# Last down projection of a two-layer encoder trunk: 8 of 22 pairs of k-tiles by Strassen's algorithm

## The chip, the cores and the metric

The kernel runs on one core of a Trainium2 chip. The core has a matrix engine (TensorE, "PE" in the profile, its weight loads "PEld"), a vector engine (VectorE, "DVE"), a scalar engine (ScalarE, "ACT"), GpSimd ("POOL"), a queue processor for DMAs (SyncE, "SP") and 16 DMA engines. Data lie in an on-chip memory of 128 partitions; TensorE writes into eight accumulator banks (PSUM) of 128 partitions by 512 float32 numbers each. The metric is the device time of one execution in microseconds (us); lower is better.

## The reference, cut to what matters

Two layers, 256 tokens, 2048 features, all in float32. Each layer ends in a gated feed-forward block; after the second layer the result is normalised. The last product and what follows it:

```python
D_MODEL, SEQ, D_FF = 2048, 256, 5632
def conv_ffn(h, w_up, conv_w, conv_b, w_down):
    ...
    return (jax.nn.gelu(acc) * b) @ w_down          # [256, 5632] @ [5632, 2048]
...
        x = x + conv_ffn(rmsnorm(x, g_ffn[l]), w_up[l], conv_w[l], conv_b[l], w_down[l])
    return rmsnorm(x, g_final)
```

## The kernel before

**Three passes for one product.** Each float32 operand is held as the exact sum of two parts of 12 significant bits, hi and lo, in a type that TensorE multiplies at full rate, and hi·hi + hi·lo + lo·hi is accumulated in PSUM. Weights come from memory as float32 and are split on the chip: `fetch` (line 98) issues one DMA of 512 KB on SP's queue, which brings a tile `raw` of two k-tiles (2 x 128 rows) by 512 columns; `split_w` rounds it on ACT into `hi` (line 108) and subtracts on DVE to get `lo` (line 109). There are five buffers for `raw`, three for `hi` and three for `lo` (`wraw`, `wspl`), seven of 128x512 for passing results (`tmp`), and an arena of 30 units of 4 KB per partition for everything that lives longer.

**The stage around the change** is the down projection of the second layer. Its left operand, `gT`, is 22 units; each holds two k-tiles of 128 features by 256 tokens, hi and lo. Tokens go on the partitions of the result: two token tiles (`t`) of 128. The 2048 output columns are taken in four blocks of 512 (`for n in range(NB)`, line 601). For each block `rows` (line 122) goes through the 22 pairs of k-tiles: one fetch, one split, then for each k-tile `j` and token tile `t` three matmuls of 128x128 by 128x512 (`rows_mms`, lines 117 to 119), 12 matmuls to a fetched tile, 1056 in the stage. A block takes two banks of the six that `acc_banks` gives out in pairs; the last block takes the two banks of `tp_bank`, and in its last four pairs the first token tile goes ahead of the second (`late=4`), so that the first one's ending lies beside the second one's products.

**Before the stage** the residual `xT`, which has features on partitions, is transposed by TensorE through the two `tp` banks (line 597), and DVE copies it to `xb` (line 598), which needs units of the arena. **After each block** DVE adds the bank to the residual (line 607), ACT sums the squares (line 609), and GpSimd multiplies with the gain of the final norm (line 611; the gain is fetched by a DMA that GpSimd issues, line 603). At the end, for each token tile, DVE finishes the mean (618), GpSimd raises it to the power -1/2 (619), DVE multiplies the last block with its gain (620), and DVE and ACT scale the four blocks and have them stored (624 to 628).

**What sets the order.** The framework puts the instructions of each engine into one list, in which they run in order; it goes by the order of the program text and by when buffers and inputs come free. An instruction waits for its inputs, and for a buffer that another one still reads.

Of the kernel before, what the change touches and what calls it, by code (L numbers as in the profile page):

```python
# [17 lines left out]
P = 128  # L18
# [23 lines left out]
def trunk_kernel(ctx, tc, x, g_mix, w_in, b_forget, g_sgu, w_spatial, b_spatial,  # L42
                 w_branch_a, w_branch_b, w_out, g_ffn, w_up, conv_w, conv_b,
                 w_down, g_final, out):
    """Every float32 product with a weight matrix runs as three float32r passes: each operand is
    the exact sum of two parts of 12 significant bits, hi and lo, and hi*hi + hi*lo + lo*hi
    is accumulated in PSUM. The RMS factor of a token is applied to the products, since it is
    one number per token; the gain goes into the transposed operand."""
# [73 lines left out]
    def rows(w2d, c0, cols, ops, late=0):  # L122
        """Products with tokens on the partitions: per token tile [token, cols]. In the last `late`
        chunks the first token tile goes ahead of the second."""
        n = len(ops)
        if late:
            acc = [tp_bank()[:, :cols] for _ in range(NT)]
        else:
            acc = acc_banks()
            acc = [acc[:, t, :cols] for t in range(NT)]  # L130
        held = []
        for m in range(n):
            hi, lo = split_w(fetch(w2d, 2 * m, 2, c0, cols), more=2 < n - m <= late)
# [38 lines left out]
    def gained(src, gains):  # L172
        """[feature, 2, token] times a gain per feature, as an operand."""
# [20 lines left out]
    def inv_rms(sq):  # L194
        """Sums of squares by feature -> [P, NT] by token, 1/sqrt(mean + eps)."""
# [9 lines left out]
    def spread(inv):  # L205
        """[P, NT] by token -> [P, 2, T], the same on every partition and twice."""
# [8 lines left out]
    def params(l):  # L215
        """Gains, conv weights and forget bias; gain() and rest() lay them out with channels on partitions."""
# [40 lines left out]
    def sgu_weights(raw):  # L257
        """The lower triangles of the spatial weights, transposed."""
# [31 lines left out]
    # ---- the first loads and products: x is transposed ahead of the chunk that needs it; until it  # L290
    # is there, products of ones keep the tensor engine's clock up ----
# [49 lines left out]
    for l in range(DEPTH):  # L341
# [191 lines left out]
        def residual(w2d, ops, sq, gains):  # L533
            """xT += w2d^T ops; its squares; its product with the gains as operands."""
# [57 lines left out]
    xb = [unit([NT, 512]) for _ in range(NB)]  # L592
    for m in range(KT // 2):
        tp = tp_bank()
        for k in range(2):
            for t in range(NT):
                nc.tensor.transpose(tp[:, (2 * t + k) * P:(2 * t + k + 1) * P], xT[m][:, k, t * P:(t + 1) * P], ident)
        nc.vector.tensor_copy(xb[m // 2][:, :, m % 2 * T:m % 2 * T + T], tp.rearrange("p (t c) -> p t c", t=NT))
    ss = small.tile([P, NT, NB], F32, tag="ss", name=nm("ss"))
    fin = small.tile([P, NT], F32, tag="fin", name=nm("fin"))  # L600
    for n in range(NB):
        gf = scratch([P, 512])
        nc.gpsimd.dma_start(gf, g_final[None, n * 512:(n + 1) * 512].broadcast_to([P, 512]))
        acc = rows(w_down[DEPTH - 1], n * 512, 512, gT, late=4 if n == NB - 1 else 0)
        for t in range(NT):
            z = xb[n][:, t, :]
            nc.vector.tensor_tensor(z, acc[t], z, op=ALU.add)
            junk = scratch([P, 512])
            nc.scalar.activation(junk, z, AF.Square, accum_out=ss[:, t, n:n + 1])
            if n < NB - 1:  # L610
                nc.gpsimd.tensor_tensor(z, z, gf, op=ALU.mult)
        if n == NB - 2:
            nc.vector.tensor_reduce(fin, ss[:, :, 0:NB - 1], axis=AX.X, op=ALU.add)
            nc.vector.tensor_scalar(fin, fin, 1.0 / D, EPS, op0=ALU.mult, op1=ALU.add)
    for t in range(NT):
        f_ = fin[:, t:t + 1]
        z = xb[NB - 1][:, t, :]
        nc.vector.scalar_tensor_tensor(f_, ss[:, t, NB - 1:NB], 1.0 / D, f_, op0=ALU.mult, op1=ALU.add)
        nc.gpsimd.tensor_tensor(f_, f_, mhalf[:, 0:1], op=ALU.pow)
        nc.vector.tensor_tensor(z, z, gf, op=ALU.mult)  # L620
# [37 lines left out]
```

## Time and profile before

| | |
|---|---|
| median of 3 runs | 2717.66 us (2717.29 to 2719.5) |
| the profiled execution, first to last instruction | 2717.0 us |
| of it, the last down projection, first to last matmul | 2465.63 to 2707.51 us |
| TensorE, DVE, ACT, GpSimd busy over the span | 99%, 60%, 48%, 19% |
| weight tiles fetched for the two down projections | 176, 512 KB each |

The profile is that of one execution. Its page gives each engine's busy time, the chain of work that ended last, and the costliest groups of instructions by line of the kernel. Answers from the trace give single instructions: start and duration in us, engine, line, operation, what it writes and reads, the shape, and in brackets how long the engine stood idle before it and what ended the wait.

### The profile page before, as it was taken

What the parts mean: (1) busy time and instruction counts of PE and PEld (TensorE: products, weight loads), DVE (VectorE), ACT (ScalarE), POOL (GpSimd) and SP (SyncE); (2) the same over time, 40 slices, a digit from 0 to 9 for tenths busy, and PEclk for the clock granted to TensorE, in tenths of its full rate; (3) what the DMA queues carried; (4) which work ended last, traced back from release to release, by engine and by line L of the source; (5) the groups of instructions that cost most, each with busy time, mean ns of one, the idle gap of its engine ahead of it and who ended that gap; (6) DMA issues with size and microseconds to landing.
All of it is one profiled execution on the core that took longest, in us unless ns stands there. A gap on an engine that the chain in (4) does not pass through costs nothing.

```text
span 2717.0 us, 38197 instructions
## 1 busy us (share of the span) xinstructions
PE 2702.2 (99%) x15120; PEld 2348.1 (86%) x15120; DVE 1640.7 (60%) x1748; ACT 1304.5 (48%) x1581; POOL 521.8 (19%) x414
## 2 busy tenths in 40 slices
PE   9999999999999999999999999999999999999998
PEld 7988888888888888888889888888888888888887
DVE  5555665666666666555555556555667676766444
ACT  5454555554444444444444545555444444444443
POOL 2200113312222222100002011133122222221000
PEclk9999999999999999999999999999999999999999
DMA  7566556656666666656665655566566666665664
GB/s 233 163 198 179 170 164 186 187 187 193 182 193 184 194 180 197 204 190 190 188 185 157 201 175 173 169 188 187 190 183 188 188 189 187 188 189 190 197 198 154
DMA packets 268219, 505.13 MB, mean 186 GB/s; under 512 B 16216, under 2 KB 33032, under 8 KB 268040
## 3 DMA queue, kind: packets, MB, share of 16 engines
q1 hardware_dynamic: 267144, 500.59, 60.8%
q8 instruction: 118, 1.93, 0.3%
q0 software_dynamic: 320, 1.05, 0.1%
q10 hardware_dynamic: 576, 1.05, 0.1%
q14 instruction: 61, 0.50, 0.1%
HBM read 500.53 MB, written 2.10 MB: 185 GB/s over the span
## 4 chain that ended last, share of the span: by engine, by line
PE 97%; POOL 1%; issue 0%; DMA 0%; ACT 0%; DVE 0%; SPq 0%; POOLq 0%; ACTq 0%
PE acc L158 54%; PE acc L160 27%; PE acc L118 4%; PE acc L117 4%; PE acc L119 4%; PE tp L119 1%; PE tp L117 1%; PE tp L118 1%; POOL sq L188 0%; POOL u L170 0%; PE tp L469 0%; PE tp L490 0%; DMA u<-in_x_dram 0%; POOL tmp L420 0%; PE tp L412 0%
## 5 line engine op out<-in xcount | busy, mean ns | idle before, releaser
L158 PE MATMUL acc<-u,hi 128*128 128x512 f32 x6336 | 2206.5, 396 | 0.0
L109 DVE TENSOR_TENSOR lo<-raw,hi 128x1024 fp32r<-128x1024 f32 (+2 forms) x959 | 1239.7, 1297 | 1013.8 <-ACT hi L108 1011.6
L160 PE MATMUL acc<-u,lo 128*128 128x256 f32 x6336 | 1738.9, 280 | 0.0
L108 ACT CAST hi<-raw 128x1024 fp32r<-128x1024 f32 (+2 forms) x959 | 992.4, 1036 | 1203.5 <-PE acc L158 934.4
L158 PEld LDWEIGHTS acc<-u,hi 128*128 128x128 f32 x6336 | 1175.3, 188 | 260.8
L160 PEld LDWEIGHTS acc<-u,lo 128*128 128x128 f32 x6336 | 1193.5, 188 | 20.9 <-issue 0.4
L118 PE MATMUL acc<-lo,u 128*128 128x512 f32 (+1 forms) x584 | 217.7, 373 | 0.9 <-DVE lo L109 0.9
L117 PE MATMUL acc<-hi,u 128*128 128x512 f32 (+1 forms) x584 | 215.7, 369 | 0.0
L119 PE MATMUL acc<-hi,u 128*128 128x512 f32 (+1 forms) x584 | 215.1, 368 | 0.0
L564 POOL TENSOR_TENSOR tmp<-tmp,bc 128x512 f32<-128x512 f32 x44 | 56.4, 1281 | 376.7 <-DVE tmp L166 351.8
L118 PEld LDWEIGHTS acc<-lo,u 128*128 128x128 f32 x584 | 110.3, 189 | 16.6 <-DVE lo L109 1.5
L117 PEld LDWEIGHTS acc<-hi,u 128*128 128x128 f32 x584 | 110.3, 189 | 15.7
L119 PEld LDWEIGHTS acc<-hi,u 128*128 128x128 f32 x584 | 110.3, 189 | 15.2
L571 DVE SCALAR_TENSOR_TENSOR tmp<-tmp,cv,tmp 128x256 f32<-128x256 f32 x176 | 118.5, 721 | 0.0
L170 POOL TENSOR_TENSOR u<-tmp,u 128x512 fp32r<-128x512 f32 x68 | 110.4, 1626 | 39.5 <-ACT u L169 39.5
L188 POOL TENSOR_TENSOR sq<-sq,tmp 128x512 f32<-128x512 f32 x28 | 40.6, 1451 | 400.8 <-ACT tmp L187 399.7
L165 ACT COPY tmp<-acc 128x512 f32<-128x512 f32 x160 | 93.4, 584 | 40.0 <-PE acc L160 40.0
L166 DVE TENSOR_TENSOR tmp<-acc,tmp 128x512 f32<-128x512 f32 x160 | 109.0, 682 | 2.1 <-ACT tmp L165 0.9
L574 POOL TENSOR_TENSOR tmp<-tmp,bc 128x512 f32<-128x512 f32 x44 | 76.3, 1734 | 119.0 <-ACT tmp L573 119.0
L503 POOL TENSOR_TENSOR tmp<-tmp,bc 128x512 f32<-128x512 f32 x32 | 41.5, 1297 | 284.6 <-DVE tmp L166 284.6
L580 POOL TENSOR_TENSOR tmp<-tmp,tmp 128x512 f32<-128x512 f32 x44 | 57.0, 1296 | 190.4 <-DVE tmp L166 164.4
L169 ACT CAST u<-tmp 128x512 fp32r<-128x512 f32 x68 | 42.0, 620 | 43.6 <-POOL tmp L528 35.7
(165 smaller groups left out, 880.2 us busy)
## 6 DMA issues: line engine op xcount, KB each, us to landing
raw<-in_w_up_dram SPq DMA_DIRECT2D x352, 512.0 KB, 4.5
raw<-in_w_in_dram SPq DMA_DIRECT2D x255, 512.0 KB, 3.8
raw<-in_w_down_dram SPq DMA_DIRECT2D x176, 512.0 KB, 4.6
raw<-in_w_out_dram SPq DMA_DIRECT2D x64, 512.0 KB, 4.7
raw<-in_w_in_dram SPq DMA_DIRECT2D x48, 344.0 KB, 3.1
raw<-in_w_branch_b_dram SPq DMA_DIRECT2D x32, 512.0 KB, 4.7
raw<-in_w_branch_a_dram SPq DMA_DIRECT2D x32, 512.0 KB, 4.3
u<-in_x_dram SPq DMA_DIRECT2D x8, 256.0 KB, 7.3
```

The source lines that it names most:

```text
L108: a = nc.scalar.copy(hi, raw)
L109: v = nc.vector.tensor_tensor(lo, raw, hi.bitcast(F32), op=ALU.subtract)
L117: m0 = nc.tensor.matmul(o, lhsT=op[:, j, 0, ts], rhs=hi[:, jw, :], start=start, stop=False)
L118: nc.tensor.matmul(o, lhsT=op[:, j, 0, ts], rhs=lo[:, jw, :], start=False, stop=False)
L119: nc.tensor.matmul(o, lhsT=op[:, j, 1, ts], rhs=hi[:, jw, :], start=False, stop=stop)
L158: nc.tensor.matmul(acc[i][:, f, :], lhsT=hi[:, j, fs], rhs=xhl, start=k == 0, stop=False, skip_group_check=True)
L160: nc.tensor.matmul(acc[i][:, f, T:2 * T], lhsT=lo[:, j, fs], rhs=xh, start=False, stop=k == nk - 1, skip_group_check=True)
L165: nc.scalar.copy(dst, a[:, :, 1, :])
L166: nc.vector.tensor_tensor(dst, a[:, :, 0, :], dst, op=ALU.add)
L170: eng.tensor_tensor(op[:, :, 1, :], src, op[:, :, 0, :].bitcast(F32), op=ALU.subtract)
L571: nc.vector.scalar_tensor_tensor(y[:, f, :], a[:, f, tap:tap + T], cv[:, tap, ft:ft + 1], y[:, f, :], op0=ALU.mult, op1=ALU.add)
L574: nc.gpsimd.tensor_tensor(y, y, inv_b, op=ALU.mult)
```

## The change

Only the last down projection changes. The four blocks of columns are taken as two groups of two (`g`), and a group needs all eight banks. For 14 of the 22 pairs of k-tiles a group does what the kernel did before, with both blocks' tiles (`ra`, `rb`) in one go: 24 matmuls, 6 on the first tile, 6 on the second, then again 6 and 6 for the second token tile. For 8 pairs (`of`: 6, 8, ..., 20) the product of the 2x2 blocks (two token tiles by two k-tiles, two k-tiles by two blocks of columns) is made by Strassen's algorithm in Winograd's form: seven products of three passes, 21 matmuls. In the first group these pairs stand at places 6, 8, ..., 20 of the loop, in the second at places 0, 2, ..., 14, each followed by a plain pair.

The sums of the left operand (`sums`) are made once per pair by GpSimd, split by ACT and DVE, and kept for the second group in four units of the arena and in the eight buffers of the residual `xT`. The sums of the weights are made for each group: `t1` on GpSimd, `rb`'s first half by a DMA that GpSimd issues and that adds to what lies in its destination, `ra`'s first half on DVE, `ra`'s second half on GpSimd. After the last Strassen pair of a group the products that aren't yet sums of the output are added to the residual. In the second group the last two pairs (`LATE`) do the first token tile ahead of the second. Docstrings and comments are taken out as well.

```diff
-    for n in range(NB):
-        gf = scratch([P, 512])
-        nc.gpsimd.dma_start(gf, g_final[None, n * 512:(n + 1) * 512].broadcast_to([P, 512]))
-        acc = rows(w_down[DEPTH - 1], n * 512, 512, gT, late=4 if n == NB - 1 else 0)
+    def sums(m, hi, lo):
+        z, s_ = scratch([P, 2, T]), scratch([P, 4, P])
+        nc.gpsimd.tensor_tensor(z, gT[m][:, :, 0, :].bitcast(F32), gT[m][:, :, 1, :].bitcast(F32), op=ALU.add)
+        nc.gpsimd.tensor_tensor(s_[:, 0, :], z[:, 0, P:T], z[:, 1, P:T], op=ALU.subtract)
+        nc.gpsimd.tensor_tensor(s_[:, 1, :], z[:, 0, 0:P], s_[:, 0, :], op=ALU.subtract)
+        nc.gpsimd.tensor_tensor(s_[:, 2, :], z[:, 0, P:T], z[:, 0, 0:P], op=ALU.subtract)
+        nc.gpsimd.tensor_tensor(s_[:, 3, :], z[:, 1, 0:P], s_[:, 1, :], op=ALU.subtract)
+        nc.scalar.copy(hi, s_)
+        nc.vector.tensor_tensor(lo, s_, hi.bitcast(F32), op=ALU.subtract)
...
+    for g in range(NB // 2):
...
+        b0, b1, b2 = (acc_banks() for _ in range(3))
+        bank = {"P1": b0[:, 0], "P2": b0[:, 1], "R7": b1[:, 0], "R3": b1[:, 1], "R6": b2[:, 0], "R5": b2[:, 1],
+                "Q4": tp_bank(), "E": tp_bank()}
...
+        out_of = {(0, 0): "P2", (0, 1): "R3", (1, 0): "Q4", (1, 1): "E"}
+
+        def plain(A, ws, t, last):
+            for q in range(2):
+                for j in range(2):
+                    go(out_of[t, q], A[t, j], ws[q][0][:, j, :], ws[q][1][:, j, :], last and j == 1)
...
+        for i, m in enumerate(order):
+            A = left(m)
+            ra, rb = (fetch(w2d, 2 * m, 2, (n0 + q) * 512, 512) for q in range(2))
+            if i not in paired:
...
+                for t in range(1 if late else NT):
+                    plain(A, ws, t, i == NG - 1)
+                continue
+            if m not in Sx:
+                Sx[m] = sums(m, *S[(m - 6) // 2])
+            s_ = Sx[m]
+            t1 = scratch([P, 512])
+            nc.gpsimd.tensor_tensor(t1, ra[:, 0, :], rb[:, 0, :], op=ALU.add)
+            nc.gpsimd.dma_start(rb[:, 0, :], rb[:, 1, :], accum_op=ALU.add)
+            hi, lo = split_w(ra)
+            go("P1", A[0, 0], hi[:, 0, :], lo[:, 0, :], i == lastS)
+            go("P2", A[0, 1], hi[:, 1, :], lo[:, 1, :])
+            nc.vector.tensor_tensor(ra[:, 0, :], ra[:, 0, :], rb[:, 0, :], op=ALU.add)
+            nc.gpsimd.tensor_tensor(ra[:, 1, :], ra[:, 1, :], ra[:, 0, :], op=ALU.add)
+            hi, lo = split_w(rb)
+            go("R7", s_[3], hi[:, 0, :], lo[:, 0, :], i == lastS)
+            go("R3", s_[4], hi[:, 1, :], lo[:, 1, :])
+            hi, lo = split_w(ra)
+            go("R6", s_[2], hi[:, 0, :], lo[:, 0, :], i == lastS)
+            go("Q4", A[1, 1], hi[:, 1, :], lo[:, 1, :])
+            hi = wspl.tile([P, 512], F32R, tag="hi", name=nm("hi"))
+            lo = wspl.tile([P, 512], F32R, tag="lo", name=nm("lo"))
+            nc.scalar.copy(hi, t1)
+            nc.gpsimd.tensor_tensor(lo, t1, hi.bitcast(F32), op=ALU.subtract)
+            go("R5", s_[1], hi, lo, i == lastS)
+            if i == lastS:
+                p1, v, z_ = scratch([P, 512]), scratch([P, 512]), scratch([P, 512])
+                nc.scalar.copy(p1, bank["P1"])
+                nc.vector.tensor_tensor(v, bank["R6"], p1, op=ALU.subtract)
+                nc.vector.tensor_tensor(z_, bank["R7"], v, op=ALU.add)
+                x = {(t, q): xb[n0 + q][:, t, :] for t in range(NT) for q in range(2)}
+                nc.gpsimd.tensor_tensor(x[0, 0], x[0, 0], p1, op=ALU.add)
+                nc.vector.tensor_tensor(x[0, 1], bank["R5"], x[0, 1], op=ALU.add)
+                nc.vector.tensor_tensor(x[1, 1], bank["R5"], x[1, 1], op=ALU.add)
+                nc.gpsimd.tensor_tensor(x[0, 1], x[0, 1], v, op=ALU.add)
+                nc.gpsimd.tensor_tensor(x[1, 0], x[1, 0], z_, op=ALU.subtract)
+                nc.gpsimd.tensor_tensor(x[1, 1], x[1, 1], z_, op=ALU.add)
...
     for t in range(NT):
         f_ = fin[:, t:t + 1]
...
+        for n in (2, 3):
+            nc.vector.scalar_tensor_tensor(f_, ss[:, t, n:n + 1], 1.0 / D, f_, op0=ALU.mult, op1=ALU.add)
         nc.gpsimd.tensor_tensor(f_, f_, mhalf[:, 0:1], op=ALU.pow)
-        nc.vector.tensor_tensor(z, z, gf, op=ALU.mult)
+        for q in range(2):
+            z = xb[2 + q][:, t, :]
+            nc.vector.tensor_tensor(z, z, gf[q], op=ALU.mult)
```

`go` calls three matmuls (hi·hi, hi·lo, lo·hi) into the named bank; `left(m)` names the hi and lo of the four blocks of the left operand.

More of the change, by code (lines that the diff above doesn't have):

```diff
@@ L598, in trunk_kernel, with left @@
         nc.vector.tensor_copy(xb[m // 2][:, :, m % 2 * T:m % 2 * T + T], tp.rearrange("p (t c) -> p t c", t=NT))
+    def left(m):
+        return {(t, j): (gT[m][:, j, 0, t * P:(t + 1) * P], gT[m][:, j, 1, t * P:(t + 1) * P])
+                for t in range(NT) for j in range(2)}
+    def sums(m, hi, lo):
[7 more added lines that the diff above has]
+        nc.vector.tensor_tensor(lo, s_, hi.bitcast(F32), op=ALU.subtract)
+        return {i + 1: (hi[:, i, :], lo[:, i, :]) for i in range(4)}
@@ new lines, in trunk_kernel, with three @@
+    NG = FT // 2
+    NS = 8
+    LATE = 2
+    S = []
+    for i in range(NS):
+        if i < 4:
+            u_ = unit([2, 4, P], F32R)
+            hi, lo = u_[:, 0], u_[:, 1]
+        else:
+            hi, lo = (xpool.tile([P, 4, P], F32R, tag=f"x{2 * (i - 4) + q}", name=nm("sx")) for q in range(2))
+        S.append((hi, lo))
+    of = {i: 6 + 2 * i for i in range(NS)}
+    Sx = {}
+    def three(bank, started, A, hi, lo, last):
+        for q, (l_, r_) in enumerate(((A[0], hi), (A[0], lo), (A[1], hi))):
+            nc.tensor.matmul(bank, lhsT=l_, rhs=r_, start=q == 0 and not started, stop=last and q == 2)
@@ L616, in trunk_kernel @@
         f_ = fin[:, t:t + 1]
-        z = xb[NB - 1][:, t, :]
-        nc.vector.scalar_tensor_tensor(f_, ss[:, t, NB - 1:NB], 1.0 / D, f_, op0=ALU.mult, op1=ALU.add)
+        for n in (2, 3):
+            nc.vector.scalar_tensor_tensor(f_, ss[:, t, n:n + 1], 1.0 / D, f_, op0=ALU.mult, op1=ALU.add)
         nc.gpsimd.tensor_tensor(f_, f_, mhalf[:, 0:1], op=ALU.pow)
-        nc.vector.tensor_tensor(z, z, gf, op=ALU.mult)
+        for q in range(2):
+            z = xb[2 + q][:, t, :]
+            nc.vector.tensor_tensor(z, z, gf[q], op=ALU.mult)
         for n in range(NB):
```

44 lines of the change are left out of this document (36 added, 8 removed).

## The prediction

> **What bounds the kernel now.** I read the page first (busy shares, the chain that ended last), then the stretches of the last down projection, then its timeline engine by engine, and last the sources of the weight fetches and of GpSimd's DMAs.
>
> ```profile
> span 2717.0 us, 38197 instructions
> PE 2702.2 (99%) x15120; PEld 2348.1 (86%) x15120; DVE 1640.7 (60%) x1748; ACT 1304.5 (48%) x1581; POOL 521.8 (19%) x414
> PE 97%; POOL 1%; issue 0%; DMA 0%; ACT 0%; DVE 0%; SPq 0%; POOLq 0%; ACTq 0%
> 2500.00:2560.00 60.00, 60.00 (x267) 49.67 (x266) 29.15 (x25) 24.44 (x26) 3.59 (x3) 1.00 0.61 199
> ```
>
> The last row is a stretch of the stage that changes (columns: stretch, its length, busy us and instructions of PE, PEld, DVE, ACT, POOL, granted clock, DMA share, GB/s). TensorE is never idle there, at full clock; DVE is busy 49%, ACT 41%, POOL 6%. So removed matmuls are worth their full time, as long as what makes their operands keeps up. What that takes is in the timeline (start, duration, instruction, idle time before it):
>
> ```profile
> 2556.09 0.39 PE L117 MATMUL acc<-hi,u 128*128 128x512 f32 x1
> 2557.91 0.39 PE L119 MATMUL acc<-hi,u 128*128 128x512 f32 x1
> 2558.13 0.39 PE L117 MATMUL acc<-hi,u 128*128 128x512 f32 x1
> 2558.81 0.39 PE L117 MATMUL acc<-hi,u 128*128 128x512 f32 x1
> ...
> 2558.33 1.05 ACT L108 CAST hi<-raw 128x1024 fp32r<-128x1024 f32 x1 [1.67 <-PE acc L119]
> ...
> 2556.70 1.23 DVE L109 TENSOR_TENSOR lo<-raw,hi 128x1024 fp32r<-128x1024 f32 x1 [1.50 <-ACT hi L108]
> 2559.42 1.23 DVE L109 TENSOR_TENSOR lo<-raw,hi 128x1024 fp32r<-128x1024 f32 x1 [1.49 <-ACT hi L108]
> ...
> 2557.95 8.53 SPq L98 DMA_DIRECT2D raw<-in_w_down_dram  x4
> DMA to landing us min/median/max: 3.6/4.5/4.9
> DMA to landing us min/median/max: 3.7/3.7/3.8
> ```
>
> Twelve matmuls take 2558.81 - 2556.09 = 2.72 us: 0.2267 us each (0.39 is the modelled length of one, they overlap). One weight tile of two k-tiles feeds 12 of them. ACT's rounding starts when TensorE lets go of a hi/lo buffer, 0.20 us after the next tile's first matmul began (2558.13 to 2558.33); DVE starts 0.04 us after ACT's end. The next fetch is issued at 2557.95, just as DVE's 2556.70 + 1.23 ends: SP waits for one of the five raw buffers, too. The two landing rows are those of the fetches over the stage and between 2556 and 2580.
>
> **What goes.** A Strassen pair is 7 products of 3 passes instead of 8: 21 matmuls, 4.76 us, for 24, 5.44 us. With 8 pairs in each of two column groups 48 matmuls go: 48 x 0.2267 = 10.88 us. Nothing else can be gained; that is 0.40% of the span.
>
> **What comes: work for the splitters.** Per Strassen pair, where two weight tiles were split, there are three splits of 128x1024, one of 128x512 (its lo on GpSimd), one add on DVE, two adds on GpSimd and one accumulating DMA. In the first group come the sums of the left operand: one 128x512 and four 128x128 operations on GpSimd, one 128x512 split.
>
> DVE alone has 3 x 1.23 + 0.69 (an add of 128x512, line 620 below) = 4.38 us of 4.76, ACT 3.5 x 1.05 = 3.7. Each would do, but DVE and GpSimd do not run side by side:
>
> ```profile
> 2529.62 1.22 DVE L109 TENSOR_TENSOR lo<-raw,hi 128x1024 fp32r<-128x1024 f32 x1
> 2532.26 2.06 DVE L109 TENSOR_TENSOR lo<-raw,hi 128x1024 fp32r<-128x1024 f32 x1 [1.43 <-ACT hi L108]
> ...
> 2530.18 3.06 POOL L611 TENSOR_TENSOR u<-u,tmp 128x512 f32<-128x512 f32 x2 [54.72 <-ACT tmp L609]
> L611 POOL TENSOR_TENSOR u<-u,tmp x6: 1283/1552/1817, 2530.2 to 2651.6; 128x512 f32<-128x512 f32 x6
> ```
>
> GpSimd's two products start inside one DVE split and last 3.06 us instead of 2 x 1.28; the next DVE split starts at 2532.26, while they run to 2533.24, and lasts 2.06 us: it ends 1.08 after them. The first product, at 1.82, ends 1.16 after DVE's. Each waits for the other to end. So their times add: 1.08 to 1.23 per split, 1.16 to 1.28 per 128x512 operation on GpSimd, 0.54 (half a split) to 0.69 for the DVE add. Strassen pairs stand between plain pairs, so I count a cycle of one of each, 45 matmuls, 10.20 us on TensorE (before: 48, 10.88). DVE plus GpSimd: 5 splits, an add, three on GpSimd: 9.42 to 10.68 us. The sums of the left operand (one 128x512, four quarters of it, one half split) add 2.86 to 3.25 us, which makes 12.28 to 13.93 if they fall into the same cycle. I take it that most don't: GpSimd is free in the first six pairs (it stood idle 54.72 us ahead of line 611), and 6 x (5.44 - 2 x 1.23) = 17.9 us without DVE hold six times 2.86. For the DVE splits that they hold up there I put 2 us (0 to 8: one product of 1.28 for each of six pairs).
>
> The Trainium skill says the same (SBUF — State Buffer, section Who interferes with whom): a DVE instruction with two SBUF inputs contends with a GpSimd instruction that reads SBUF, and the loser is blocked for the whole instruction. The trace agrees (2.06 us for 1.23).
>
> **What comes: a loop through five raw buffers.** The cycle fetches four tiles: two plain ones, then `ra`, `rb`. The fetch of the next `rb` comes after that of the next plain two and of the next `ra`, so all of five buffers are held until this `rb` is split. Between these two fetches lies a whole chain, none of which TensorE covers: fetch, GpSimd's `t1`, the accumulating DMA, ACT's rounding, DVE's lo. The nearest rows for the DMA are the 256 KB loads of g_final that GpSimd issues (issue, then landing); the floor is the 8 KB load of g_mix:
>
> ```profile
> L603 POOL DMA_DIRECT2D tmp<-in_g_final_dram x4: 579/579/754, 2457.4 to 2593.0; - x4
> DMA to landing us min/median/max: 3.4/4.1/5.9
> r<-in_g_mix_dram SPq DMA_DIRECT2D x2, 8.0 KB, 1.6
> ```
>
> I take 4.1, the median of the same size and queue (1.6 to 8.2: as short as the small load, or twice the load, since the destination is read as well). Then 3.7 + 1.28 + 4.1 + 1.05 + 1.23 and five hand-overs of 0.04 = 11.56 us. With the 4.9 us fetch, 1.82, 5.9 and a blocked 2.06 it would be 15.9. The loop is longer than 10.20 us by 1.36, and TensorE waits for it at the second weight tile of each Strassen pair: 15 times (8 + 8 pairs, less the first), 20.4 us. Behind the wait stand on ACT the rounding of the next tiles, on DVE the add and their lo, on GpSimd `ra`'s second sum, so nothing slips past.
>
> By the Trainium skill (DMA: Bandwidth & Descriptors, section Anatomy of one DMA — SWDGE (gpsimd) path) such a transfer takes 2.0 us and its bytes at 436 GB/s, an estimate of 2.6 us for 256 KB, by which the loop would be 10.06 us and hidden. The g_final rows, 3.4 to 5.9, lie above it.
>
> **What moves: banks at the start, the end.** Group one needs all eight banks, two of them from the two that transpose the residual:
>
> ```profile
> 2471.37 1.27 DVE L598 COPY u<-tp 128x512 f32<-128x512 f32 x2
> ...
> 2488.95 1.28 DVE L598 COPY u<-tp 128x512 f32<-128x512 f32 x2
> 2476.13 1.03 PE L597 MATMUL tp<-ident,x 128*128 128x128 f32 x8
> 2465.63 0.40 PE L117 MATMUL acc<-hi,u 128*128 128x512 f32 x1
> ```
>
> The stage began at 2465.63, but the eight copies end at 2490.23. Until then the second token tile has no bank. Meanwhile TensorE has 12 + 6 matmuls of the first token tile, until the three hi/lo buffers are full (4.08 us), and the three batches of transposes left (1.03 each): to 2472.8. The six copies left after 2472.64, if they follow at once (0.64 each), end at 2476.5. I take 4 us of waiting (0 to 18, the latter at the old spacing).
>
> Between the groups I put nothing: the first Strassen pair uses no bank that the last six matmuls write, and the others are read while these run (without that cover, one DVE add, 0.69 us). The additions that turn the seven products into sums of the output (on GpSimd four of 1.28) lie beside the plain pair that follows, 5.44 us; without it they would cost their 5 us once. At the end one more product per token tile stands on DVE:
>
> ```profile
> 2707.93 0.69 DVE L607 TENSOR_TENSOR u<-tp,u 128x512 f32<-128x512 f32 x1 [1.82 <-PE tp L119]
> 2709.49 0.69 DVE L620 TENSOR_TENSOR u<-u,tmp 128x512 f32<-128x512 f32 x1
> 2709.65 0.94 POOL L619 TENSOR_TENSOR fin<-fin,mhalf 128x1 f32<-128x1 f32 x1 [4.46 <-DVE fin L618]
> 2710.62 0.88 DVE L624 TENSOR_SCALAR u<-u,fin 128x512 f32<-128x512 f32 x2 [0.45 <-POOL fin L619]
> ```
>
> Line 620 twice ends at 2710.87, 0.25 us after GpSimd's power: 0.25 us (0 to 0.69). The weights split ahead for the last two pairs cost nothing: one tile per six matmuls, 1.36 us against 1.23, as in the old ending.
>
> **Sum.** 2717.0 - 10.88 + 20.4 (loop) + 4 (start) + 2 (sums) + 0.25 (end) = 2732.8. The median of the runs, 2717.66, lies 0.66 above the profiled span: 2733.4, so 2733, slower by 0.57%. Less than 0.2% (5.4 us) I call no change: about what can be told here.
>
> **Rivals.**
> *The loop is hidden.* Place: the accumulating DMA. If it lands within 10.20 - (11.56 - 4.1) = 2.7 us, TensorE stays the bound. For it: source and target are both on the chip, and the floor is 1.6. Against it: 3.4 is the quickest of its size in this queue, and it reads its target as well. One wait stays: the first plain tile takes the buffer of `rb`, free 12 matmuls into the Strassen pair; 9 matmuls and the first of its own later (2.27 us) its lo is due, but ACT and DVE need 0.20 + 1.05 + 0.04 + 1.23 + 0.04 = 2.56. That is 0.3 x 16 = 4.8 us. 2717.66 - 10.88 + 4.8 = 2711.6, with the start's 4 us 2715.6. Chance 0.35: faster in 0.2, no change in 0.15.
> *Engines that block each other become the bound.* Sums of the left operand stay in their cycles, 13.93 us each, and the DMA takes 5.9, the loop 13.36: -10.88 + 7 x 3.73 + 8 x 3.16 + 4 = +44.5, 2762. For it: the lock above; against it: GpSimd's idle time beforehand. Chance 0.13.
> *The banks hold up the start at the old spacing:* 14 us more than the forecast, 2747. Against it: TensorE then has nothing else to do than transpose. Chance 0.05.
>
> **Numbers.** The forecast has 0.47, its own range is 2720 to 2750: with the quickest rows (3.6, 3.4, 1.22) the loop is 10.75 us, 12 us less in all, and with a fetch of 4.5 it is 12.36, 12 us more. Some 0.06 of it lies under 2723. Faster by over 0.2%: 0.2; within: 0.21; slower: 0.59. The range reaches down to the hidden loop and up to nearly the mutual block: 2708 to 2758.
>
> **What would show it.** 1008 matmuls in the stage; TensorE idle some 1.4 us before the second weight tile of each Strassen pair, ended by DVE's lo, behind ACT's rounding that waited for the accumulating DMA; its landing near 4.1 us. DVE splits of 2 us beside GpSimd's adds. An idle stretch of TensorE within 10 us of the stage's start. Wrong it is if the DMA lands within 2.7 us, or if `rb` is in place well before ACT asks for it.

## The result and the profile after

The changed kernel takes 2809.76 us (median of 4 runs, 2802.65 to 2811.37) beside 2717.89 us for the one before (4 runs, 2717.29 to 2719.5): a ratio of 1.0331, 95% interval 1.0316 to 1.0345. It is 92 us slower. The forecast was 2733 and the range ended at 2758. The profiled execution spans 2807.5 us, 90.5 more than before.

The page of the changed kernel, in the order in which the page before was read:

```profile
PE 2727.0 (97%) x15072; PEld 2354.4 (84%) x15072; DVE 1714.6 (61%) x1800; ACT 1333.9 (48%) x1623; POOL 653.9 (23%) x524
PEclk9999999999999999999999999999999999999889
PE 88%; DMA 5%; POOL 2%; DVE 2%; issue 1%; ACT 1%; SPq 0%; POOLq 0%; ACTq 0%; DVEq 0%
raw<-raw POOLq DMA_DIRECT2D x16, 256.0 KB, 5.7
```

48 matmuls are gone (15120 to 15072), but TensorE's share of the chain that ended last fell from 97% to 88%: the missing 9% went to the DMAs, GpSimd, DVE and ACT. The clock row (granted clock in 40 equal slices of the span, 9 is 90% or more) says where: of the last three slices two are below 9. And the new DMA takes 5.7 us to land, not 4.1.

Then the stretches of the last down projection of the changed kernel (columns as in the prediction: busy us of PE, PEld, DVE, ACT, POOL, granted clock, DMA share, GB/s). The first lies ahead of the Strassen pairs, the second in the first group's, the last in the second group's:

```profile
2470.00:2500.00 30.00, 29.63 (x136) 24.09 (x137) 16.22 (x17) 11.69 (x12) 8.86 (x11) 1.00 0.57 168
2500.00:2550.00 50.00, 38.52 (x149) 28.58 (x147) 30.20 (x21) 18.14 (x20) 31.04 (x27) 0.93 0.50 144
2640.00:2755.00 115.00, 88.61 (x318) 67.50 (x319) 60.10 (x46) 42.79 (x46) 43.77 (x32) 0.84 0.52 146
```

Where 50 us of plain pairs would hold 220 matmuls (50 / 0.2267), there are 149. No engine is full: TensorE 77%, GpSimd 62%, DVE 60%, ACT 36%, and 144 GB/s are moved where it was 199. That is the picture of a loop: every member waits for another one. The waits of the stage name the members (us in total, times, longest):

```profile
ACT hi L108 <- DMA raw<-raw: 81.3, 14, 8.6
POOL raw L693 <- DVE raw L692: 75.8, 16, 7.0
DVE raw L692 <- DMA raw<-raw: 52.4, 14, 5.1
PEld acc L635 <- ACT hi L108: 47.1, 16, 12.3
```

ACT waits for the accumulating DMA 14 times, once per Strassen pair but for two; DVE waits for it too, and GpSimd waits behind DVE. The chain of waits over one turn in the second group (start, us, what) is closed, and TensorE isn't on it:

```profile
2644.14 1.05 ACT hi L108
...
2645.21 1.99 DVE lo L109
...
2647.22 3.70 DMA raw<-in_w_down_dram
...
2651.08 2.16 POOL tmp L687
2653.24 0.29 issue
...
2653.54 5.28 DMA raw<-raw
...
2658.97 1.06 ACT hi L108
...
2660.05 2.15 DVE lo L109
```

From one rounding of `rb` to the next are 2658.97 - 2644.14 = 14.83 us, where TensorE needs 10.20. Line 692, the add on DVE that comes once per Strassen pair, measures all turns, one row for each group:

```profile
L692 DVE TENSOR_TENSOR raw<-raw,raw x8: 683/691/693, 2501.3 to 2617.3; 128x512 f32<-128x512 f32 x8
L692 DVE TENSOR_TENSOR raw<-raw,raw x8: 691/692/693, 2644.1 to 2751.0; 128x512 f32<-128x512 f32 x8
```

Seven turns of 116.0 / 7 = 16.57 us, then seven of 106.9 / 7 = 15.27, and 26.8 us between the groups. Over the 10.20 us of TensorE this is 7 x 6.37 + 7 x 5.07 + 16.6 = 96.7 us; less the 10.9 us of removed matmuls, 85.8. The stage became 91.7 us longer (from its first to its last matmul 241.9 us before, 333.6 after), so 6 us are left for what lies ahead of the first add and behind the last.

### The profile page after: what moved, and what is told of

It reads as the page before. It is cut to its first block, busy times and chain, and to the rows that moved or that the text cites. A ratio compares the mean times of both kernels' runs of the same rounds, so it can differ in the third digit from the quotient of the medians.

```text
span 2807.5 us, 38439 instructions
## 1 busy us (share of the span) xinstructions
PE 2727.0 (97%) x15072; PEld 2354.4 (84%) x15072; DVE 1714.6 (61%) x1800; ACT 1333.9 (48%) x1623; POOL 653.9 (23%) x524
## 3 DMA queue, kind: packets, MB, share of 16 engines
q10 hardware_dynamic: 576, 1.05, 0.1%
## 4 chain that ended last, share of the span: by engine, by line
PE 88%; DMA 5%; POOL 2%; DVE 2%; issue 1%; ACT 1%; SPq 0%; POOLq 0%; ACTq 0%; DVEq 0%
PE acc L158 52%; PE acc L160 27%; DMA raw<-raw 3%; DMA raw<-in_w_down_dram 2%; PE acc L118 2%; PE acc L119 2%; PE acc L117 2%; DVE lo L109 1%; PE acc L635 1%; PE tp L635 1%; ACT hi L108 1%; POOL tmp L610 0%; POOL tmp L687 0%; POOL u L170 0%; PE tp L469 0%
## 5 line engine op out<-in xcount | busy, mean ns | idle before, releaser
L109 DVE TENSOR_TENSOR lo<-raw,hi 128x1024 fp32r<-128x1024 f32 (+2 forms) x975 | 1287.0, 1325 | 971.4 <-ACT hi L108 968.2
L108 ACT CAST hi<-raw 128x1024 fp32r<-128x1024 f32 (+2 forms) x975 | 1007.7, 1035 | 1239.6 <-PE acc L158 934.1
L635 PE MATMUL acc<-hi,u 128*128 128x512 f32 x344 | 126.7, 416 | 24.3 <-ACT hi L108 24.2
L118 PE MATMUL acc<-lo,u 128*128 128x344 f32 (+1 forms) x320 | 114.3, 357 | 0.9 <-DVE lo L109 0.9
L117 PE MATMUL acc<-hi,u 128*128 128x344 f32 (+1 forms) x320 | 112.5, 352 | 0.0
L119 PE MATMUL acc<-hi,u 128*128 128x344 f32 (+1 forms) x320 | 111.8, 349 | 0.0
L635 PEld LDWEIGHTS acc<-hi,u 128*128 128x128 f32 x344 | 69.5, 202 | 43.1 <-ACT hi L108 28.5
L635 PE MATMUL tp<-hi,u 128*128 128x512 f32 x248 | 91.1, 408 | 0.2 <-DVE u L600 0.2
L635 PE MATMUL acc<-lo,u 128*128 128x512 f32 x172 | 72.5, 422 | 11.8 <-DVE lo L109 11.8
```

Of the source, the lines that this page charges most:

```text
L108: a = nc.scalar.copy(hi, raw)
L109: v = nc.vector.tensor_tensor(lo, raw, hi.bitcast(F32), op=ALU.subtract)
L117: m0 = nc.tensor.matmul(o, lhsT=op[:, j, 0, ts], rhs=hi[:, jw, :], start=start, stop=False)
L118: nc.tensor.matmul(o, lhsT=op[:, j, 0, ts], rhs=lo[:, jw, :], start=False, stop=False)
L119: nc.tensor.matmul(o, lhsT=op[:, j, 1, ts], rhs=hi[:, jw, :], start=False, stop=stop)
L635: nc.tensor.matmul(bank, lhsT=l_, rhs=r_, start=q == 0 and not started, stop=last and q == 2)
```

## Experiments

Each ratio is to the kernel before on the same chip, whose median lay between 2717.62 and 2718.55 us, so that medians of different experiments can be compared, too. Most medians are of two runs. "Turn" is the distance of line 692's adds as above (694 where the edit moves it by two lines), first group / second group. The changed kernel has 16.57 / 15.27.

**Is it the grouping?** All pairs plain, in the same two groups of two blocks:

```diff
-            paired = {6 + 2 * i: 6 + 2 * i for i in range(NS)}
+            paired = {}
...
-            paired = {2 * i: 6 + 2 * i for i in range(NS)}
+            paired = {}
```

> All 22 pairs plain, in the new grouping of two blocks of columns with eight banks; no Strassen pair. Prices the regrouping alone. Theory of the loop (weights wait for a raw buffer, the accumulating DMA and the engines behind it): without Strassen pairs there is no loop, TensorE at full rate, 1056 matmuls, 2718 to 2724. Rival, the grouping itself stalls (six matmuls on a tile instead of twelve, all banks taken, nothing spare at the change of group): 2735 or more.

2720.44 us, ratio 1.0009 (0.9999 to 1.0018). Its stage:

```profile
2480.00:2700.00 220.00, 219.29 (x967) 180.95 (x966) 104.04 (x88) 88.43 (x90) 7.96 (x6) 1.00 0.61 192
```

TensorE is full, so eight banks at once, two tiles of weights at once and the new ending cost about 2.6 us (-0.3 to 4.9 by the interval). All the rest comes with the Strassen pairs.

**Is it the accumulating DMA?** Two kernels. In the first DVE makes the sum instead:

```diff
-            nc.gpsimd.dma_start(rb[:, 0, :], rb[:, 1, :], accum_op=ALU.add)
+            nc.vector.tensor_tensor(rb[:, 0, :], rb[:, 0, :], rb[:, 1, :], op=ALU.add)
```

> The sum of rb by DVE (0.69 us) instead of the accumulating DMA (issue to landing about 5.5 us). Theory of the loop: it shortens by about 5 us per cycle, to about 10.5 us, close to TensorE's 10.2: 2809 less 15 x 4.8 = 2737, full clock nearly everywhere. Rival, DVE and GpSimd blocking each other set the cycle: with one DVE operation more the cycle can't fall under 13 to 14 us in the first group and 11.5 in the second: 2755 or more.

2760.83 us, 1.0158 (1.0137 to 1.0178): 49 us won back, but not the 73 that my theory of the loop asked for; the rival's number (2755 or more) is what came. In the second, the DMA stays and copies without adding (this leaves the addition out):

```diff
-            nc.gpsimd.dma_start(rb[:, 0, :], rb[:, 1, :], accum_op=ALU.add)
+            nc.gpsimd.dma_start(rb[:, 0, :], rb[:, 1, :])
```

> The changed kernel with a plain DMA of the same 256 KB in the same queue instead of the accumulating one; it leaves out the addition in rb. If adding is what makes the transfer long (5.7 us from issue to landing, where 256 KB loads took 4.1 to 4.4), it lands about 1.5 us sooner, and each of 15 loops is that much shorter: about 2787. If it's the queue and the chip's other traffic, nothing changes: 2805 to 2812.

2785.47 us, 1.0248 (1.0229 to 1.0266). How long the two DMAs take to land, the changed kernel first, then the copy with its adds of line 692:

```profile
DMA to landing us min/median/max: 3.3/5.7/6.9
```

```profile
DMA to landing us min/median/max: 2.3/4.1/5.3
L692 DVE TENSOR_TENSOR raw<-raw,raw x8: 683/693/693, 2502.3 to 2606.8; 128x512 f32<-128x512 f32 x8
L692 DVE TENSOR_TENSOR raw<-raw,raw x8: 691/692/693, 2632.5 to 2726.2; 128x512 f32<-128x512 f32 x8
```

The copy lands 1.6 us sooner, and the turns are 14.93 / 13.39, shorter by 1.64 and 1.88. A transfer whose shortening shortens the turn one for one lies on the path that sets it. Single turns scatter, though (14.2 to 17.9 us in the changed kernel), and the mean of one group moves by up to 1.1 us between kernels with the same code in it (15.43 in one further down, for 16.57), so that the stronger evidence is the median: 24 us less, 1.6 for each of 15 turns. It also shows that 4.1 us, which I took for the accumulating DMA, is what a plain transfer of this size takes: the adding costs 1.6 on top.

**Is it the number of raw buffers?** Two kernels with four Strassen pairs, which leaves room in the arena, and one with a sixth raw buffer. First four pairs, their sums of the left operand all in the residual's buffers, weights through the five buffers:

```diff
-    NS = 8
+    NS = 4
```

> Four Strassen pairs instead of eight (left sums in the old buffers of the residual), weights fetched as before into the five raw buffers. Theory of the loop: 3 cycles of about 16.5 and 3 of 15.3 and the change of group at 27 stay: 2718 - 5.4 + 3 x 6.3 + 3 x 5.1 + 16.6 = 2763. Rival (the four pairs in the arena matter, or the clock): not half the loss.

2765.67 us, 1.0175 (1.0155 to 1.0196): half the pairs, half the loss (48 of 92). Then the same with the Strassen pairs' tiles in arena units of their own:

```diff
-    def fetch(w2d, k0, nk, c0, cols):
-        raw = wraw.tile([P, nk, cols], F32, tag="raw", name=nm("raw"))
+    def fetch(w2d, k0, nk, c0, cols, own=False):
+        raw = unit([nk, cols]) if own else wraw.tile([P, nk, cols], F32, tag="raw", name=nm("raw"))
```

> As the run with four pairs, but the weights of Strassen pairs are fetched into four arena units of their own, so that the next pair's chain can start before this one's is split. Theory of the loop: the waits inside the groups go, what stays is part of the change of group: 2716 to 2730, against 2763. Rival, DVE and GpSimd block each other: 12.3 to 13.9 us a cycle in the first group stay, 2735 to 2745. Rival, the clock or the DMA's own time: as with four pairs, 2755 to 2765.

2743.58 us, 1.0094 (1.0079 to 1.0109): 22 us less by nothing but where the tiles lie (and the plain tiles have the five buffers for themselves). The row at the head of the list of waits in the changed kernel, ACT's rounding behind the accumulating DMA, first in the one, then in the other, where the tiles are arena units (`u`) and one such wait is left, that at the change of group:

```profile
ACT hi L108 <- DMA raw<-raw: 41.3, 8, 8.3
```

```profile
ACT hi L108 <- DMA u<-u: 9.5, 1, 9.5
```

Last, eight pairs with a sixth raw buffer, for which two of the `tmp` buffers go:

```diff
-    wraw = ctx.enter_context(tc.tile_pool(name="wraw", bufs=5))
+    wraw = ctx.enter_context(tc.tile_pool(name="wraw", bufs=6))
...
-    tmp = ctx.enter_context(tc.tile_pool(name="tmp", bufs=7))
+    tmp = ctx.enter_context(tc.tile_pool(name="tmp", bufs=5))
```

> The changed kernel with six raw buffers instead of five; for the room, five buffers of 128x512 for passing results instead of seven. Nothing else moves: same DMA, same GpSimd and DVE work. Theory of the loop: rb of the next pair is fetched when the second plain tile is split, not when this pair's rb is split, some 9 us sooner, so that fetch, t1 and accumulating DMA no longer hang on the split before them. Cycles fall from 15.3 and 16.6 us to what DVE and GpSimd allow, 11.5 to 14: 2745 to 2775. Rival, the DMA's time or the two engines are the bound whatever the buffers: 2795 or more. If five passing buffers are too few, the stages before the last one show it.

2769.5 us, 1.019 (1.0161 to 1.022): 40 us of the 92 go with one buffer more, while the accumulating DMA stays.

```profile
L692 DVE TENSOR_TENSOR raw<-raw,raw x8: 680/684/693, 2500.1 to 2597.6; 128x512 f32<-128x512 f32 x8
L692 DVE TENSOR_TENSOR raw<-raw,raw x8: 691/692/693, 2626.4 to 2709.0; 128x512 f32<-128x512 f32 x8
```

Its second group's stretch, columns as above:

```profile
2630.00:2710.00 80.00, 73.81 (x296) 58.22 (x296) 52.34 (x41) 38.13 (x40) 35.27 (x26) 0.93 0.69 203
```

TensorE is busy 92% of it, where it was 77%. The turns are 13.93 / 11.80: almost those of DVE's own sum, 13.57 / 11.83. So the loop through five buffers is shown from three sides (a shorter transfer in it, none in it, one buffer more), and behind it lies something else at about 13.7 / 11.8.

**What is the second limit?** My rival in the runs was that DVE and GpSimd, which block each other, are simply full. From the kernel in which DVE makes the sum, one operation of 1.8 us on GpSimd that is off the loop through the raw buffers is taken away (this leaves the lo part of `t1` out, its hi stands in):

```diff
             nc.scalar.copy(hi, t1)
-            nc.gpsimd.tensor_tensor(lo, t1, hi.bitcast(F32), op=ALU.subtract)
+            lo = hi
```

> As the run with rb's sum on DVE, but the lo of t1 is left out (its hi is used in its place): one GpSimd operation of 1.8 us less per Strassen pair, which is not in the loop through the raw buffers. Theory: once the DMA is gone, DVE and GpSimd, who block each other, are the bound (97% of the first group's cycles one or the other is busy, 90% of the second's): cycles shorter by 1.2 us or so, 2761 - 16 x 1.2 = 2742, not under 10.2 us a cycle. Rival, the loop is still the bound: 2758 to 2763.

2756.87 us, 1.0141 (1.0123 to 1.016): 4 us less, not the 19 that two full engines would have given. The second group's turns went from 11.77 to 11.33 us (the last six of each). So the sum of the two engines' work is not what sets the turn. And with all sums of the left operand ahead of the groups:

```diff
+    for i in range(NS):
+        Sx[of[i]] = sums(of[i], *S[i])
     for g in range(NB // 2):
```

> As the run with rb's sum on DVE, with all left sums ahead of the first group. Theory of the two engines: the first group's cycles fall from 13.9 to the second's 11.7 us: 7 x 2.2 = 15 us, less some 5 us for the start (4.3 us in the run with the sums first): 2745 to 2752. Rival, the loop: 2758 to 2763.

2755.94 us, 1.0138 (1.0119 to 1.0157), between the ranges of the theory (2745 to 2752) and of the rival (2758 to 2763), so it decides for neither. Its turns in the first group are 82.2 / 7 = 11.74 us, like the second group's:

```profile
L694 DVE TENSOR_TENSOR raw<-raw,raw x8: 691/692/693, 2509.9 to 2592.1; 128x512 f32<-128x512 f32 x8
```

Thus the left operand's sums make up all of the difference between the groups' turns, 1.8 us each on average; but the first add comes 7.5 us later (2502.4 before, 2509.9 now): more than half of the 7 x 1.83 us that the turns win is lost where the sums now stand. The same edit in the changed kernel:

> All eight sums of the left operand stand ahead of the first group in the program text, instead of beside their pairs. In the changed kernel GpSimd does the first one of the next pair (2.3 us beside DVE) between t1 and the issue of the accumulating DMA, in the first group. Theory of the loop: cycles of the first group fall from 16.6 to the 15.3 of the second, 7 x 1.3 = 9 us: 2800, some of it lost where the sums hold DVE up in the first six pairs. Rival (the place of the sums doesn't matter, DVE and GpSimd have the same work): 2809.

2795.9 us, 1.0286 (1.0267 to 1.0305): 14 us won, 4 more than expected. The turns of its first group come down to 99.2 / 7 = 14.17, its first add comes 8.5 us later. Those of the second group, whose code is the same, are shorter as well, 102.7 / 7 = 14.67 for 15.27, within the scatter named above. One row of it, for the 20 us in which GpSimd makes the sums:

```profile
2470.00:2490.00 20.00, 15.35 (x67) 11.63 (x67) 17.03 (x13) 6.37 (x8) 19.38 (x23) 0.91 0.27 87
```

GpSimd is busy all the time, DVE for 17.03 us with 13 instructions, 1.31 each; TensorE gets 67 matmuls done where 88 fit.

**The change of group.** At 2632.99 the first group's last matmul starts, at 2645.23 the second group's first. GpSimd's timeline between them, in the changed kernel:

```profile
2633.45 1.28 POOL L728 TENSOR_TENSOR u<-u,tmp 128x512 f32<-128x512 f32 x1
2634.66 1.17 POOL L643 DMA_DIRECT2D tmp<-in_g_final_dram  x2
2635.81 1.31 POOL L728 TENSOR_TENSOR u<-u,tmp 128x512 f32<-128x512 f32 x1
2637.03 1.31 POOL L687 TENSOR_TENSOR tmp<-raw,raw 128x512 f32<-128x512 f32 x1
2638.25 2.51 POOL L728 TENSOR_TENSOR u<-u,tmp 128x512 f32<-128x512 f32 x2
2640.68 0.97 POOL L688 DMA_DIRECT2D raw<-raw  x1
```

The second group begins with a Strassen pair. Its `t1` and the issue of its DMA stand in GpSimd's list behind the four products that end the first group (line 728) and the gain's fetch (643). Only at 2640.68 is the DMA issued, 3.3 us later it lands. With four plain pairs at the head of the second group:

```diff
-            paired = {2 * i: 6 + 2 * i for i in range(NS)}
+            paired = {2 * i + 4: 6 + 2 * i for i in range(NS)}
```

> In the second group the Strassen pairs stand at places 4, 6, ..., 18 instead of 0, 2, ..., 14. TensorE idled 12.25 us at the change of group, while GpSimd finished the first group's sums and fetched the gain ahead of t1 and of the DMA's issue. Behind four plain pairs (21.8 us) that is covered: 12 us less and the slow matmuls after it, 2795 to 2798. Rival, the loop just moves along (the buffers were full anyway): 2805 or more.

2790.88 us, 1.0268 (1.0249 to 1.0286): 19 us won, somewhat more than expected, but its two runs lie 8 us apart, and the slower one is at the expected 2795; the profile is that of the faster one. No stretch over 1.6 us without a matmul is left between the groups. From the last add of the first group to the first of the second are 38.3 us, for 141 matmuls that take 32.0: 6.3 us too many are left of 16.6. Its turns are shorter too, 15.43 / 14.56, with the same code in them; the cause is open.

**Is there a version that gains?** Four pairs in buffers of their own, two plain pairs between two Strassen pairs, sums ahead, four plain pairs at the head of the second group:

```diff
-            paired = {6 + 2 * i: 6 + 2 * i for i in range(NS)}
+            paired = {6 + 3 * i: 6 + 3 * i for i in range(NS)}
...
-            paired = {2 * i: 6 + 2 * i for i in range(NS)}
+            paired = {4 + 3 * i: 6 + 3 * i for i in range(NS)}
```

> Everything together: four Strassen pairs with weight buffers of their own, two plain pairs between them, left sums ahead, the second group starting with four plain pairs. TensorE's share falls by 5.4 us; a cycle is 69 matmuls, 15.6 us, for which DVE and GpSimd together have 11.8 to 13.3. Theory of the loop and of the two engines that block each other: both have room, only hand-overs (0.3 to 0.9 us each Strassen pair) and the 2.5 us of the regrouping are left: 2718 to 2726. Rival, a Strassen pair costs its stall wherever it stands (slow matmuls after each gap): 2730 or more.

2729.86 us, 1.0044 (1.003 to 1.0058): a miss, my theory had at most 2726, and it lies just under the rival's 2730. In its turns TensorE is full; it loses at the stage's start, where GpSimd makes the sums, and at the second group's first Strassen pair. So in the last version the sums come after the first pair, and each Strassen pair's fetch, `t1` and DMA stand two pairs ahead in the text:

```diff
+            if i + 2 in paired:
+                m2 = paired[i + 2]
+                ra, rb = (fetch(w2d, 2 * m2, 2, (n0 + q) * 512, 512, own=True) for q in range(2))
+                t1 = scratch([P, 512])
+                nc.gpsimd.tensor_tensor(t1, ra[:, 0, :], rb[:, 0, :], op=ALU.add)
+                nc.gpsimd.dma_start(rb[:, 0, :], rb[:, 1, :], accum_op=ALU.add)
+                early[i + 2] = ra, rb, t1
```

> Four Strassen pairs with weight buffers of their own and two plain pairs between them, and now the fetch of their weights, t1 and the accumulating DMA stand two pairs earlier in the program text; the left sums stand behind the first pair. In the spaced version the fetch stood in SP's queue behind the plain ones, so that the first pair of the second group waited 2 us, and the start 4.5 us behind DVE's part of the left sums. Theory of the loop: with the chain of 12 us off the path nothing is left but the regrouping's 2.5 us: 2718 + 2.5 - 5.4 = 2715, up to 2720. Rival, DVE and GpSimd hold the splits up wherever the pair stands: 2724 or more.

2726.89 us, 1.0031 (1.0018 to 1.0043): the rival's number, not that of my theory. Three stretches of it:

```profile
2470.00:2490.00 20.00, 17.10 (x76) 12.76 (x77) 15.16 (x13) 7.70 (x10) 19.37 (x22) 1.00 0.60 195
2490.00:2550.00 60.00, 59.96 (x262) 48.49 (x261) 37.23 (x31) 28.39 (x29) 15.24 (x13) 1.00 0.73 218
2610.00:2630.00 20.00, 17.76 (x77) 13.67 (x76) 11.60 (x9) 7.68 (x8) 8.64 (x6) 1.00 0.77 234
```

The middle one holds Strassen and plain pairs, and TensorE is full at full clock, with the accumulating DMA in it. The first one, with the sums, loses 2.9 us, the last one, the head of the second group, 2.2 us. At the end of each group, in the stretches 2550 to 2570 and 2630 to 2680, 0.9 us more are lost (19.12 of 20 and 49.12 of 50 us busy). 24 matmuls less are worth 5.4 us; these four together, 6.9 us, eat them up. With the 2.6 us of the grouping that explains 4 of the 8 us by which this version is slower; the rest is open. No version beat the kernel before.

## Why the prediction was wrong

**Right: what goes, and the mechanism.** 48 matmuls went. The loop through five raw buffers is what sets the time: its members stand on the chain as the prediction lists them, fetch, `t1`, DMA, rounding, lo, and each of the ways to loosen it won 22 to 49 us. 14 of the 16 Strassen pairs wait at the place that was named, at ACT's rounding of `rb` behind the DMA.

**Wrong: the loop's length.** This is the step that failed, "five hand-overs of 0.04 = 11.56 us". One turn of the second group, term by term:

| term | forecast | measured |
|---|---|---|
| fetch | 3.7 | 3.70 |
| `t1` on GpSimd | 1.28 | 2.16 |
| until the DMA is issued | 0.04 | 0.30 |
| accumulating DMA | 4.1 | 5.28 (median of all 5.7) |
| rounding on ACT | 1.05 | 1.06 |
| lo on DVE | 1.23 | 2.15 |

Each measured term comes from the turn quoted above; with 0.35 us for the other hand-overs they make 15.00 us, for 11.56. Three of the forecast's terms are too small, by 1.2 for the DMA and by 0.9 for each of the two operations on the engines that block each other. I had seen the lock of DVE and GpSimd and had counted it as a sum of work, but not as a delay inside the chain. In the turn quoted `t1` starts at 2651.08, when the fetch lands, while DVE is in a split (2650.86 to 2652.09), and DVE's lo of `rb` starts while GpSimd is in line 693, since both follow the landing of the same DMA. DVE's timeline and GpSimd's, in the changed kernel:

```profile
2659.01 0.69 DVE L692 TENSOR_TENSOR raw<-raw,raw 128x512 f32<-128x512 f32 x1 [3.22 <-DMA raw<-raw]
2660.05 2.14 DVE L109 TENSOR_TENSOR lo<-raw,hi 128x1024 fp32r<-128x1024 f32 x1 [0.35 <-ACT hi L108]
```

```profile
2659.84 1.26 POOL L693 TENSOR_TENSOR raw<-raw 128x512 f32<-128x512 f32 x1 [5.40 <-DVE raw L692]
```

Line 693 ends at 2661.10; the split that starts within it, at 2660.05, ends 1.09 us after that, at 2662.19, about its own undisturbed length later. That fits the rule of the Trainium skill (SBUF — State Buffer, section Who interferes with whom) that the ports that DVE and GpSimd share are an exclusive lock. The prediction had quoted the long row of each kind, and the loop that it made of them, 15.9 us, lies between the two groups' turns, 15.27 and 16.57. That it fits so well is partly luck: its fetch (4.9) is longer than the one measured in that turn (3.70), and it has no sum of the left operand in it. It stood there as an outer bound and was then dropped: the forecast's own range used 10.75 to 12.36, and the upper end of 2758 took 13.93 as the longest turn. 15 x (15.9 - 10.20) = 85.5 us in place of the 20.4 would have given 2798.

**Wrong: the price of the DMA.** 4.1 us was the median of loads that add nothing; the copy shows the adding's 1.6 us. By the Trainium skill (DMA: Bandwidth & Descriptors, section Anatomy of one DMA — SWDGE (gpsimd) path) my estimate was 2.6 us. The runs do not agree: of the plain copies the quickest took 2.3, but half of them 4.1 or more, in a stage whose weight fetches keep the DMA engines half busy; the measured number decides.

**Wrong: the change of group at nothing.** It has 12.24 us between two matmuls. I had looked only at banks. The list of GpSimd wasn't followed across the boundary, where what ends one group stands ahead of what starts the next. Four plain pairs there take away some 10 us of the 16.6 by which that turn was too long.

**Wrong: the sums of the left operand "mostly" ahead.** Only two of the eight stand in GpSimd's list ahead of the first add (line 610 at 2457.41 and 2494.23); the other six lie in the first six turns of the first group. GpSimd's timeline in one of them, in the changed kernel:

```profile
2557.62 2.03 POOL L687 TENSOR_TENSOR tmp<-raw,raw 128x512 f32<-128x512 f32 x1 [1.16 <-DMA raw<-in_w_down_dram]
2559.60 2.30 POOL L610 TENSOR_TENSOR tmp<-u 128x512 f32<-128x512 f32 x1
2561.84 0.86 POOL L688 DMA_DIRECT2D raw<-raw  x1
```

The next pair's sum (line 610) slips between `t1` and the issue of the DMA, so that 2.3 us are put into the loop itself (1.3 in one of the six). The six turns take 16.84 us on average, the seventh, without a sum, 14.94: 1.9 us. With all of them ahead of the groups that group's turn was 2.4 us shorter (14.17); both are rough, by the scatter of the turns. I had asked whether such a sum would fill the engine, not whether it would stand ahead of something urgent.

**Right or small.** The start cost little: 29.63 of 30 us are busy in the first stretch above, not the 4 us that I put there. The end is as before: 9.6 us from the start of the last matmul to the end of the span, for 9.5.

**The sum again.** Forecast 20.4 us for the loop's excess, measured 96.7 (80.1 in 14 turns, 16.6 at the change of group); removed matmuls 10.9 both times. For start, sums and end I had 6.25 us, and 6 are left in the measured sum, but that is luck, since they are something else: some 2 us at the start, and some 4 us behind the last add, where TensorE idles 2.86 and 1.38 us once more in the last Strassen pair. The whole miss is in the first term.

**What lies behind the loop.** With the loop loosened, a turn takes 11.8 us (13.7 with a left sum), not 10.20. The traces show that this isn't one limit. With DVE's own sum and the left sums ahead, the turn from the add at 2662.70 to the next at 2674.44 is a closed round of 11.74 us through three engines. GpSimd's timeline in it:

```profile
2663.53 2.15 POOL L695 TENSOR_TENSOR raw<-raw 128x512 f32<-128x512 f32 x1 [3.86 <-ACT hi L108]
2667.42 1.74 POOL L705 TENSOR_TENSOR lo<-tmp,hi 128x512 fp32r<-128x512 f32 x1 [1.74 <-ACT hi L704]
2669.12 2.30 POOL L689 TENSOR_TENSOR tmp<-raw,raw 128x512 f32<-128x512 f32 x1
```

The add on DVE lets line 695 start, which lasts 2.15 us beside a split. ACT then rounds `ra` (2665.71) and `t1` (2666.66), GpSimd makes the lo of `t1` (line 705), and the next pair's `t1` (line 689) stands behind it in GpSimd's list. At 2671.45 DVE sums the next `rb`, then does the two splits that stand ahead of the next add, which starts as they end. No step starts more than 0.15 us after the one before it has ended.

Without the lo of `t1` another round comes up, the one through the five raw buffers: from the end of one split of `rb` (2678.70) to the end of the next (2689.80) are 11.10 us, made up of the fetch until `t1` starts (4.4), `t1` (1.79), and on DVE, one behind the other, the sum (0.69), two splits (2.35), the add (0.69) and `rb`'s split (1.23). That is why 1.8 us less on GpSimd won 0.4 a turn: the one round lies close behind the other. With the sixth buffer it is a third place. In the second group's stretch ACT never waits for the accumulating DMA any more, but TensorE's longest waits there (6.0 us, three times; it is busy 73.81 of 80 us) are for line 703, the lo of `t1`, ahead of which GpSimd's list now has the next pair's `t1` and the issue of its DMA. That the turn is 11.8 us there, too, looks like chance. No run loosened any of these three, so that what would come behind them is open.

## What to carry to other kernels

A buffer that is held until the end of a chain makes a loop: go round it with the durations that its members have while the other members run (blocked ones included), and with what stands ahead of each in its engine's list, not with their undisturbed ones. Removing 0.4% of the span's time from the busiest engine did not pay here for a detour over two engines that lock each other out and a DMA; the best of the versions tried still lost 0.3%. And at each boundary of a stage read the list of the engine that issues DMAs: what closes the old stage stands ahead of what opens the new one.

## What the runs showed of the chip

**The granted clock is halved after waits of some microseconds.** The prediction knew only a granted clock of 1.00. In the changed kernel it is 0.93 and 0.84 in the two Strassen stretches, and the timeline of TensorE, after a wait of 4.14 us, shows how; below it stands the stretch that holds the slow matmuls, with a granted clock of 0.50:

```profile
2603.50 0.50 PE L635 MATMUL acc<-hi,sx 128*128 128x512 f32 x1 [4.14 <-ACT hi L108]
...
2608.71 0.63 PE L635 MATMUL acc<-lo,sx 128*128 128x512 f32 x1
2609.14 0.63 PE L635 MATMUL acc<-hi,sx 128*128 128x512 f32 x1
...
2611.51 0.39 PE L635 MATMUL acc<-lo,sx 128*128 128x512 f32 x1
2611.73 0.39 PE L635 MATMUL acc<-hi,sx 128*128 128x512 f32 x1
```

```profile
2608.00:2611.00 3.00, 3.00 (x9) 2.32 (x8) 1.23 (x1) 1.39 (x2) 1.43 (x1) 0.50 0.67 246
```

Matmuls stand 0.43 us apart, and some microseconds later 0.22 again (granted clock 1.00 between 2614 and 2618). Counted over the single matmuls of the stage, some 130 start 0.33 to 0.55 us after the one before, in all 24 us more than at 0.2267; the longer distances add up to 76 us more. The Trainium skill (TensorE: Matmul & The Clock Gate, section Part 1: The HAM clock gate) describes a gate that halves the clock after an idle window and opens it after a busy one; the spacing, 0.43 for 0.22, agrees. What these 24 us cost could not be separated: TensorE is not on the chain in the turns, so they may fill time that would have been idle.

**The adding in a DMA has a price,** 1.6 us for 256 KB on the chip (5.7 us for 4.1), and its issue holds GpSimd 0.88 us instead of 0.55, both from the rows of line 688 in the changed kernel and in the copy:

```profile
L688 POOL DMA_DIRECT2D raw<-raw x16: 847/878/966, 2495.5 to 2744.0; - x16
```

```profile
L688 POOL DMA_DIRECT2D raw<-raw x16: 553/553/577, 2496.6 to 2722.7; - x16
```
